# Interleaved gate and up weights, layer norms on one engine, and a later start of the PLE product in a 32-expert block

## The chip, the cores and the metric

The program runs on one core of one Trainium2 chip. Its time is the device time of one execution, in microseconds. The kernel before takes 2994.66 us, the median of three runs (2991.4 to 3000.03). The engines are named as in the profile: PE is TensorE, DVE is VectorE, ACT is ScalarE, POOL is GpSimd, SP is SyncE, which here only issues loads.

## The reference

Sequence length 256, width 2048, fp32. A first block (a mixer of an RWKV7 and an mLSTM branch, a mixture of experts, two layer norms) is followed by two further layers and a final norm. The change lies in the first block behind the mixer:

```
x = layer_norm(ALPHA * x + mix @ w_out, ln1_w, ln1_b)
moe = hier_moe(x, ...)          # 4 groups x 8 experts, top 1 group, top 2 experts
    # per expert: (silu(x_e @ w_gate) * (x_e @ w_up)) @ w_down, weighted, added back
ple = sigmoid(x @ w_pg) * (p @ w_ple)
x = layer_norm(ALPHA * x + moe + ple, ln2_w, ln2_b)
```

with `layer_norm(x) = (x - mean) * rsqrt(var + 1e-5) * w + b`. `w_gate` and `w_up` are 2048x512 for each of the 32 experts, `w_down` is 512x2048, `w_pg` 2048x2048, `w_ple` 256x2048. The weights of the experts alone are 403 million bytes.

## The kernel before, in words

Values that must keep fp32 accuracy outside the experts are split into a high and a low part (`split`, L316 the cast on ACT, L317 the difference on DVE or POOL), and a product is three matmuls (L220 to L222): high by high, low by high, high by low. A stream object (`st`) loads weight pieces of half a MB (`wraw`, L133), splits them (`whi`, `wlo`) and runs such products; `st.weave` mixes them with another generator's work.

The stages around the change: `out1` computes the output projection `mix @ w_out` from 32 loads (830 to 912 us), and adds x and the first statistics (L1082, L1083). `layer_norm` then works on two token tiles in four chunks of 512 columns: ACT scales and shifts (L1053), DVE multiplies by the weight (L1054), and POOL or DVE adds the bias (L1055). Each finished chunk is transposed (L1070), split (`xh`, `xl`), and multiplied by the router's weights (L1122 to L1124). `route` is a chain of small DVE operations; three small matmuls (L1201 to L1203) count the tokens of each expert, and a one-hot matrix (`oh`) follows.

`experts` works on four experts at a time: gather matmuls (L1327, `oh` by the rows' high part `zh` and low part `zl`) put up to 64 token rows of each expert in `xg`; then, per expert, gate and up (L1431), the activation, the down product (L1395) and the way back to the tokens (L1358, L1359). The weights come in blocks of 1 MB, twelve per expert (four gate, four up, four down), in the order that `expert_order` yields. A ring of eight buffers (`ew`) holds them, and two further blocks lie in `res`, free at that time. The ring's first eight blocks are issued from ACT's queue during `out1`; all others from SP's, each as soon as its buffer is free. A fp32 matmul of the program is recorded as two instructions. PLE (L220 to L222 on `xh`) is woven between the experts' steps, from the first expert on. At expert 24 stands a branch for tokens beyond the 64 rows (L1232), which is not taken. Behind the last expert come the second layer norm and the first norm of the next layer (L1684, `rdg`, a diagonal matrix of scales; L1691).

The order of the work within each engine is set when the program is built, by a scheduler that goes by buffers and the code's order; each queue then runs its list in order.

Of the kernel before, what the change touches and what calls it, by code (L numbers as in the profile page):

```python
# [9 lines left out]
F32 = mybir.dt.float32  # L10
F32R = mybir.dt.float32r
I32 = mybir.dt.int32
AF = mybir.ActivationFunctionType
# [252 lines left out]
class Ker:  # L266
# [767 lines left out]
    def ln_scale(self, pool, st, i, eps):  # L1034

        nc = self.nc
        mv = pool.tile([128, 2], F32, name="bmv")
        nc.vector.bn_aggr(mv, st[:, i])
        rs = pool.tile([128, 2], F32, name="brs")
        nc.vector.tensor_scalar_add(rs[:, 0:1], mv[:, 1:2], eps)  # L1040
        nc.gpsimd.tensor_tensor(rs[:, 0:1], rs[:, 0:1], self.mhalf, op=OP.pow)  # L1041
        nc.vector.scalar_tensor_tensor(rs[:, 1:2], mv[:, 0:1], -1.0, rs[:, 0:1], op0=OP.mult, op1=OP.mult)
        return rs[:, 0:1], rs[:, 1:2]

    def layer_norm(self, W2, z, st, w, b, eps, then):

        nc = self.nc
        scales = [self.ln_scale(W2, st, i, eps) for i in range(2)]
        for i, (rs, nm) in enumerate(scales):
            for c in range(4):  # L1050
                s = slice(512 * c, 512 * c + 512)
                v = z[:, i, s]
                nc.scalar.activation(v, v, AF.Identity, scale=rs, bias=nm)  # L1053
                nc.vector.tensor_mul(v, v, w[:, s])  # L1054
                (nc.vector if c % 2 else nc.gpsimd).tensor_add(v, v, b[:, s])  # L1055
                then(i, c)
# [153 lines left out]
    def overflow(self, EP, W2, acc, xh, xl, wt, pos, dram, hh, hl):  # L1210
# [21 lines left out]
        with tc.If(any_over > 0):  # L1232
            nc.sync.dma_start(dram.rearrange("e p a -> p a e"), wo)
            with tc.For_i(0, 32, 1) as e:
                gu = lambda n, c: lambda k0, kn: lambda raw: nc.sync.dma_start(
                    raw, A[n][bass.ds(e, 1), k0 // KCH, :, :, c:c + 256].rearrange("o p k n -> (o p) k n"))
                dn = lambda c, kp: lambda raw: nc.sync.dma_start(
# [4 lines left out]
                for c in range(0, 512, 256):  # L1242
                    h = EP.tile([128, 512], F32, name="plg0", bufs=1).rearrange("p (a s) -> p a s", a=2)

                    def ev_g(i, ps):
                        nc.scalar.activation(h[:, i], ps, AF.Silu)

                    def ev_u(i, ps):
                        nc.vector.tensor_mul(h[:, i], h[:, i], ps)
                        self.split(hh[:, i], hl[:, i], h[:, i])  # L1250

                    def ev_d(i, c, ps):
                        v = acc.t[:, i, 512 * c:512 * c + 512]
                        nc.vector.scalar_tensor_tensor(v, ps, wc[:, i:i + 1], v, op0=OP.mult, op1=OP.add)

                    st.cols_of(KT, 0, 256, xh, xl, ev_g, gu("w_gate", c))
                    st.cols_of(KT, 0, 256, xh, xl, ev_u, gu("w_up", c))
                    st.run()
                    st.rows(None, c // 256, 2, 0, D, hh, hl, ev_d, load=dn)
                    st.run()  # L1260

    def expert_order(self):
# [12 lines left out]
        for e in range(32):  # L1275
            for k in range(4):
                yield A["w_gate"][e, k]
                yield A["w_up"][e, k]
                if k == 1 and e:
                    yield from down(e - 1)  # L1280
# [12 lines left out]
    def load_expert(self, eng=None, t=None):  # L1293
        src = next(self.worder)
        t = self.wring.tile([128, 2048], F32, name="ew") if t is None else t
        v = t.rearrange("p (k n) -> p k n", n=src.shape[2])
        if src.shape[1] == 4:
            (eng or self.nc.sync).dma_start(t, src.rearrange("p k n -> p (k n)"))
        else:
            (eng or self.nc.sync).dma_start(v, src)  # L1300
        return v

    def experts(self, pool, W2, zp, x1, acc, wt, pos, bst):
# [6 lines left out]
        def load():  # L1310
            return self.wready.pop(0) if self.wready else self.load_expert()
# [98 lines left out]
        for e in range(32):  # L1410
            j = e % 4
            if j == 0:
                oh, xg, step = gather(e)
                step(0)
                if e == 0:
                    self.st.after = None
                sw = slot_weights(e, oh)
                yield
                if e == 24:
                    yield from self.start_overflow()  # L1420
# [4 lines left out]
            for k0 in range(0, KT, 4):  # L1425
                wg = load()
                wu = load()
                for w, ps in ((wg, acc_t[:, 0:256]), (wu, acc_t[:, 256:512])):
                    for k in range(4):
                        for g in range(2):  # L1430
                            nc.tensor.matmul(ps[64 * g:64 * g + 64], xg[:, k0 + k, j], w[:, k, 256 * g:256 * g + 256],  # L1431
                                             start=w is wg and k0 + k == 0, stop=k0 + k == KT - 1,
                                             tile_position=(0, 64 * g), skip_group_check=True)
                if j == 0 and k0 + 4 < KT:
# [608 lines left out]
def body(tc, A, out):  # L2043
# [13 lines left out]
    with ExitStack() as top:  # L2057
# [84 lines left out]
        with ExitStack() as pb:  # L2142
            psum(pb, 4)
            rp = pool(pb, "route")
            st.open(pool(pb, "ringB"), raw=2, split=2)
            xp = pool(pb, "xB")
            xh, xl = xp.tile([128, KT, S], F32R, name="xh"), xp.tile([128, KT, S], F32R, name="xl")
            ph, pl = xp.tile([128, 2, S], F32R, name="ph"), xp.tile([128, 2, S], F32R, name="pl")
            EP = pool(pb, "ex1")
            zh = xp.tile([128, 2, D], F32R, name="zh")  # L2150
            with ExitStack() as e:
# [14 lines left out]
                K.layer_norm(W2, z, bst, lw, lb, 1e-5, then)  # L2166
                st.after = [K.last_split]
                for c in range(4):
                    for i in range(2):
                        v = slice(512 * c, 512 * c + 512)  # L2170
                        nc.scalar.copy(zh[:, i, v], z[:, i, v])
                res = []
                st.weave(K.route(rp, R, lg, res))
                wt, pos = res
            K.ple(acc, EP, xh, xl, ph, pl)
            W2 = pool(pb, "ex2", bufs=2)
            zl = W2.tile([128, 2, D], F32R, name="zl", bufs=1)
            acc.x1 = zh, zl
            for c in range(4):
                for i in range(2):  # L2180
                    v = slice(512 * c, 512 * c + 512)
# [63 lines left out]
def prep(inp):  # L2245
# [41 lines left out]
    for n in ("w_out", "w_pg", "w_ple"):  # L2287
        a[n] = _by_rows(f(n)[0])
    for n in ("w_gate", "w_up"):
        a[n] = f(n)[0].reshape(32, 4, 4, 128, 512).transpose(0, 1, 3, 2, 4)  # L2290
    w = f("w_in_even_2")[0]
# [40 lines left out]
```

## Time and profile before

| | |
|---|---|
| median of three runs | 2994.66 us |
| profiled execution | 2988.51 us, its span 2986.6 us |
| PE busy | 2805.2 us (94%) |
| DVE, ACT, POOL busy | 55%, 38%, 17% |
| DMA over the span | 744.96 MB, 249 GB/s mean |
| DMA slices at 0.9 or more | from about 950 to 1970 us, the expert stage |

PE's busy time includes matmuls that are spread out by their operands, so the 94% is not an engine at its peak. The row of DMA slices shows the stage that the change is about: outside it, the DMA engines are busy for one to eight tenths, inside it for nine or more. In a row of windows the columns are the stretch, its length, the busy time of PE, PE's weight loads, DVE, ACT and POOL (with the number of instructions), PE's granted clock as a share of full speed, the share in which the 16 DMA engines were busy, and GB/s. In a row of the timeline they are the start, the time taken, the engine (SPq is SP's queue of loads), the line, the operation, what it writes and reads with shapes, how many follow each other, and in brackets the idle time before with the instruction or load that ended it.

### The profile page before, as it was taken

What the parts mean: (1) busy time and instruction counts of PE and PEld (TensorE: products, weight loads), DVE (VectorE), ACT (ScalarE), POOL (GpSimd) and SP (SyncE); (2) the same over time, 40 slices, a digit from 0 to 9 for tenths busy, and PEclk for the clock granted to TensorE, in tenths of its full rate; (3) what the DMA queues carried; (4) which work ended last, traced back from release to release, by engine and by line L of the source; (5) the groups of instructions that cost most, each with busy time, mean ns of one, the idle gap of its engine ahead of it and who ended that gap; (6) DMA issues with size and microseconds to landing.
All of it is one profiled execution on the core that took longest, in us unless ns stands there. A gap on an engine that the chain in (4) does not pass through costs nothing. (4 is left out here: it accounts for less than half of the span.)

```text
span 2986.6 us, 42995 instructions
## 1 busy us (share of the span) xinstructions
PE 2805.2 (94%) x16907; PEld 2068.6 (69%) x16907; DVE 1654.7 (55%) x2642; ACT 1138.7 (38%) x1959; POOL 516.2 (17%) x530
## 2 busy tenths in 40 slices
PE   8999899988998999999999899869889999999998
PEld 7877787876886555555555445447667787888887
DVE  7876865888666322222232222169999665555555
ACT  5443434555544212112112111044545554555454
POOL 4111102277103000000000000026675200000000
PEclk9999899999999999999999999989999999999999
DMA  6442142475684999999999999945555454555554
GB/s 195 135 132 71 53 147 96 163 254 198 225 310 175 404 415 398 419 417 386 419 419 413 418 396 419 419 186 185 165 168 166 170 202 157 186 180 188 181 180 166
DMA packets 170526, 744.96 MB, mean 249 GB/s; under 512 B 20544, under 2 KB 35408, under 8 KB 120784
## 3 DMA queue, kind: packets, MB, share of 16 engines
q1 hardware_dynamic: 162800, 719.09, 64.4%
q10 hardware_dynamic: 6624, 19.93, 1.8%
q0 software_dynamic: 896, 3.15, 0.4%
q8 instruction: 135, 2.21, 0.3%
q14 instruction: 71, 0.58, 0.1%
HBM read 727.40 MB, written 14.70 MB: 248 GB/s over the span
## 5 line engine op out<-in xcount | busy, mean ns | idle before, releaser
L155 PE MATMUL acc<-xx,whi 128*128 128x512 f32 (+2 forms) x2624 | 945.3, 403 | 16.9 <-ACT whi L316 11.3
L317 DVE TENSOR_TENSOR wlo<-wraw,whi 128x1024 fp32r<-128x1024 f32 x559 | 717.3, 1285 | 365.3 <-ACT whi L316 362.1
L159 PE MATMUL acc<-xx,wlo 128*128 128x256 f32 (+2 forms) x2624 | 729.3, 288 | 44.6 <-DVE wlo L317 44.5
L316 ACT CAST whi<-wraw 128x1024 fp32r<-128x1024 f32 x564 | 589.3, 1046 | 459.8 <-PE acc L222 224.2
L155 PEld LDWEIGHTS acc<-xx,whi 128*128 128x128 f32 (+2 forms) x2624 | 490.4, 190 | 123.8 <-ACT whi L316 11.8
L159 PEld LDWEIGHTS acc<-xx,wlo 128*128 128x128 f32 (+2 forms) x2624 | 499.5, 190 | 82.4 <-DVE wlo L317 62.2
L1431 PE MATMUL acc<-ew,xg 128*64 128x256 f32 x4064 | 482.2, 385 | 23.6 <-DMA ew<-in_w_gate 10.7
L1431 PEld LDWEIGHTS acc<-ew,xg 128*64 128x64 f32 x4064 | 282.1, 137 | 202.2 <-issue 34.8
L1369 DVE TENSOR_TENSOR z<-mx,z 64x512 fp32r<-64x512 f32 x128 | 86.7, 688 | 429.5 <-ACT z L1368 427.9
L1395 PE MATMUL mx<-ew,eht 128*64 128x512 f32 x992 | 228.6, 598 | 13.8 <-DMA ew<-in_w_down 13.8
L1368 ACT CAST z<-mx 64x512 fp32r<-64x512 f32 x128 | 74.1, 580 | 380.8 <-PE mx L1395 363.4
L1041 POOL TENSOR_TENSOR brs<-brs,mhalf 128x1 f32<-128x1 f32 x4 | 2.7, 671 | 1097.4 <-DVE brs L1040 1097.4
L1395 PEld LDWEIGHTS mx<-ew,eht 128*64 128x64 f32 x992 | 66.5, 136 | 142.9 <-issue 105.9
L166 ACT COPY halves<-acc 128x256 f32<-128x256 f32 x204 | 74.3, 366 | 215.2 <-PE acc L155 213.4
L221 PE MATMUL acc<-wlo,xx 128*128 128x512 f32 x256 | 102.1, 399 | 3.9 <-DVE wlo L317 3.9
L1376 DVE SCALAR_TENSOR_TENSOR eh<-eh,sw,acc 128x256 f32<-128x256 f32 x32 | 15.3, 480 | 159.7 <-ACT eh L1375 159.7
L222 PE MATMUL acc<-whi,xx 128*128 128x512 f32 x256 | 101.3, 396 | 0.0
L221 PE MATMUL acc<-wlo,oo 128*128 128x512 f32 x256 | 100.0, 391 | 0.0
L222 PE MATMUL acc<-whi,oo 128*128 128x512 f32 x256 | 99.5, 389 | 0.0
L220 PE MATMUL acc<-whi,xx 128*128 128x512 f32 x256 | 95.8, 397 | 0.0
L220 PE MATMUL acc<-whi,oo 128*128 128x512 f32 x256 | 93.1, 390 | 0.6 <-DVE res L1930 0.6
L168 DVE TENSOR_TENSOR halves<-halves,acc 128x256 f32<-128x256 f32 x148 | 61.1, 413 | 56.5 <-ACT halves L166 55.9
(614 smaller groups left out, 4056.1 us busy)
## 6 DMA issues: line engine op xcount, KB each, us to landing
ew<-in_w_down SPq DMA_DIRECT2D x128, 1024.0 KB, 14.3
ew<-in_w_gate SPq DMA_DIRECT2D x123, 1024.0 KB, 13.5
ew<-in_w_up SPq DMA_DIRECT2D x123, 1024.0 KB, 13.4
wraw<-in_wo_qkz SPq DMA_DIRECT2D x96, 512.0 KB, 3.3
wraw<-in_w_g SPq DMA_DIRECT2D x64, 512.0 KB, 3.3
wraw<-in_w_rkv SPq DMA_DIRECT2D x52, 512.0 KB, 3.6
wraw<-in_we_u SPq DMA_DIRECT2D x48, 512.0 KB, 3.5
wraw<-in_w_out SPq DMA_DIRECT2D x32, 512.0 KB, 5.2
```

Of the source, the lines that this page charges most:

```text
L155: nc.tensor.matmul(ps, p.hi[:, k], x.both(kk), start=kk == 0, stop=last, skip_group_check=True)
L159: nc.tensor.matmul(ps[:, 0:S], p.lo[:, k], x.h[:, kk], start=False, stop=False, skip_group_check=True)
L166: nc.scalar.copy(v, ps[:, S:])
L220: nc.tensor.matmul(acc[i], xh[:, kk, m], p.hi[:, k], start=kk == 0, stop=False)
L221: nc.tensor.matmul(acc[i], xh[:, kk, m], p.lo[:, k], start=False, stop=False)
L222: mm = nc.tensor.matmul(acc[i], xl[:, kk, m], p.hi[:, k], start=False, stop=last)
L316: self.last_split = self.nc.scalar.copy(hi, src).ins
L317: (eng or self.nc.vector).tensor_sub(lo, src, hi.bitcast(F32))
L1368: m = nc.scalar.copy(o[:, 0], v).ins
L1369: nc.vector.tensor_sub(o[:, 1], v, o[:, 0].bitcast(F32))
L1395: nc.tensor.matmul(py[b][64 * g:64 * g + 64, :], ht[:, k % 2, k // 2], wd[:, 0, c:c + 512], start=k == 0, stop=k == 3, tile_position=(0, 6 ...
L1431: nc.tensor.matmul(ps[64 * g:64 * g + 64], xg[:, k0 + k, j], w[:, k, 256 * g:256 * g + 256], start=w is wg and k0 + k == 0, stop=k0 + k == ...
```

## The change

The gate and up weights of an expert are stored as eight blocks of 1 MB, each with two slices of 128 rows and, for either half of the columns, 256 gate columns beside 256 up columns. A matmul covers 512 columns instead of 256, and there are half as many. The layer norm is two DVE operations for each chunk, `(x - mean) * w` and `(...) * rs + b`; the rows' low parts `zl` come from DVE too. PLE is started at the third expert, with its buffers opened there. Two more blocks are loaded ahead, into a pool `pre`. The branch stands at expert 28.

```diff
-        for i, (rs, nm) in enumerate(scales):
+        for i, (mean, rs) in enumerate(scales):
             for c in range(4):
...
-                nc.scalar.activation(v, v, AF.Identity, scale=rs, bias=nm)
-                nc.vector.tensor_mul(v, v, w[:, s])
-                (nc.vector if c % 2 else nc.gpsimd).tensor_add(v, v, b[:, s])
+                nc.vector.scalar_tensor_tensor(v, v, mean, w[:, s], op0=OP.subtract, op1=OP.mult)
+                nc.vector.scalar_tensor_tensor(v, v, rs, b[:, s], op0=OP.mult, op1=OP.add)
                 then(i, c)
...
         for e in range(32):
-            for k in range(4):
-                yield A["w_gate"][e, k]
-                yield A["w_up"][e, k]
-                if k == 1 and e:
+            for k in range(8):
+                yield A["w_gu"][e, k]
+                if k == 3 and e:
                     yield from down(e - 1)
...
         for e in range(32):
             j = e % 4
+            if e == 2:
+                self.start_ple()
             if j == 0:
                 oh, xg, step = gather(e)
                 step(0)
-                if e == 0:
-                    self.st.after = None
...
-                if e == 24:
+                if e == 28:
                     yield from self.start_overflow()
...
-                wg = load()
-                wu = load()
-                for w, ps in ((wg, acc_t[:, 0:256]), (wu, acc_t[:, 256:512])):
-                    for k in range(4):
-                        for g in range(2):
-                            nc.tensor.matmul(ps[64 * g:64 * g + 64], xg[:, k0 + k, j], w[:, k, 256 * g:256 * g + 256],
...
+                for k in range(k0, k0 + 4):
+                    w = load() if k % 2 == 0 else w
+                    for g in range(2):
+                        nc.tensor.matmul(acc_t[64 * g:64 * g + 64], xg[:, k, j], w[:, k % 2, 512 * g:512 * g + 512],
+                                         start=k == 0, stop=k == KT - 1, tile_position=(0, 64 * g))
...
-            st.open(pool(pb, "ringB"), raw=2, split=2)
+            px = ExitStack()
+            pre = pool(px, "pre", bufs=2, side="right")
+            K.wready += [K.load_expert(t=pre.tile([128, 2048], F32, name="pre")) for _ in range(2)]
...
-                st.after = [K.last_split]
                 for c in range(4):
                     for i in range(2):
                         v = slice(512 * c, 512 * c + 512)
-                        nc.scalar.copy(zh[:, i, v], z[:, i, v])
+                        K.split(zh[:, i, v], zl[:, i, v], z[:, i, v])
...
-            K.ple(acc, EP, xh, xl, ph, pl)
...
-                    nc.gpsimd.tensor_sub(zl[:, i, v], z[:, i, v], zh[:, i, v].bitcast(F32))
+            def start_ple():
+                px.close()
+                st.open(pool(pb, "ringB", side="right"), raw=2, split=2)
+                K.ple(acc, EP, xh, xl, ph, pl)
...
-            for _ in range(2):
-                with tc.issue_after(K.mark):
-                    st.step()
```

On SP's queue, from the loads of the output projection (`w_out`) to the first loads of the experts, the order before was:

```order
L133 DMA wraw<-in_w_out 128x1024 x27
L1298 DMA res<-in_w_gate 128x2048
L1298 DMA res<-in_w_up 128x2048
L133 DMA wraw<-in_w_pg 128x1024 x8
L1298 DMA ew<-in_w_gate 128x2048
L1298 DMA ew<-in_w_up 128x2048
L1300 DMA ew<-in_w_down 128x2048 x4
```

In the changed kernel it is:

```order
L133 DMA wraw<-in_w_out 128x1024
L1301 DMA pre<-in_w_gu 128x2048 x2
L133 DMA wraw<-in_w_out 128x1024 x26
L1301 DMA res<-in_w_gu 128x2048 x2
L1304 DMA ew<-in_w_down 128x2048 x4
L1301 DMA ew<-in_w_gu 128x2048 x4
L133 DMA wraw<-in_w_pg 128x1024 x2
```

The two new blocks stand ahead of 26 loads of `w_out`, and the eight first pieces of `w_pg`, which stood ahead of the ring's refill, stand behind eight blocks of it.

The same queue at the end of the experts, with the second norm's weights (`lnw`, `lnb`), before:

```order
L1298 DMA ew<-in_w_up 128x2048
L1300 DMA ew<-in_w_down 128x2x1024 x4
L1031 DMA lnw<-in_ln_w 128x2048
L1031 DMA lnb<-in_ln_b 128x2048
L133 DMA wraw<-in_we_u 128x1024
```

In the changed kernel, behind the branch (L1230):

```order
L1230 UNCONDITIONAL_BRANCH
L1031 DMA lnw<-in_ln_w 128x2048
L1031 DMA lnb<-in_ln_b 128x2048
L1301 DMA ew<-in_w_gu 128x2048 x5
L133 DMA wraw<-in_we_u 128x1024 x3
L1301 DMA ew<-in_w_gu 128x2048 x3
L1304 DMA ew<-in_w_down 128x2048 x4
```

The two loads moved from behind the last expert load to a place ahead of the last four experts' blocks.

On PE, from the last of the router's logits (`lt`) through the counts (`chosen`) to the first gathers (`oh`), the order before ends so:

```order
L220 MATMUL acc<-whi,xh 128x512 x2
L1327 MATMUL mx<-oh,zh 128x256 x2
L1340 MATMUL mx<-wt,oh 64x1 x2
L1327 MATMUL mx<-oh,zh 128x256
L1340 MATMUL mx<-wt,oh 64x1 x4
L1327 MATMUL mx<-oh,zl 128x256
```

In the changed kernel:

```order
L1126 MATMUL mx<-ident,lt 128x36
L1199 MATMUL mx<-chosen,low 128x32
L1200 MATMUL mx<-chosen,ones 128x32
L1201 MATMUL mx<-chosen,low 128x32
L1331 MATMUL mx<-oh,zh 128x256
L1331 MATMUL mx<-oh,zl 128x256
```

Of the PLE matmuls (L220 to L222), 50 stood between the logits and the first gathers; none does now, and the next instruction behind the logits is the first count.

## Rows read from the trace of the kernel before

**Rows 1.** Windows of the expert stage.

```profile
955.00:990.00 35.00, 35.00 (x293) 24.82 (x292) 5.78 (x8) 6.92 (x11) 5.97 (x4) 1.00 0.84 316
1105.00:1145.00 40.00, 39.50 (x247) 22.85 (x247) 11.23 (x14) 7.53 (x11) 0.00 (x0) 1.00 0.97 373
1145.00:1335.00 190.00, 183.37 (x1259) 106.78 (x1257) 49.08 (x76) 33.77 (x55) 0.00 (x0) 1.00 1.01 419
1335.00:1390.00 55.00, 55.00 (x337) 31.01 (x335) 14.99 (x20) 15.96 (x21) 0.00 (x0) 1.00 0.94 371
1390.00:1600.00 210.00, 203.92 (x1420) 118.57 (x1418) 54.31 (x84) 40.65 (x65) 0.00 (x0) 1.00 1.01 419
1711.00:1714.00 3.00, 2.66 (x10) 1.14 (x10) 0.00 (x0) 0.00 (x0) 0.00 (x0) 0.50 1.01 412
1720.00:1725.00 5.00, 5.00 (x42) 2.68 (x38) 0.00 (x0) 0.00 (x0) 0.00 (x0) 1.00 0.31 95
1725.00:1955.00 230.00, 206.27 (x1415) 107.44 (x1414) 49.94 (x82) 28.57 (x54) 0.00 (x0) 0.99 1.01 419
```

**Rows 2.** Timeline of PE at the end of the expert stage.

```profile
1949.43 1.95 PE L1431 MATMUL acc<-ew,xg 128*64 128x256 f32 x16 [0.55 <-DMA ew<-in_w_gate]
1951.94 1.95 PE L1431 MATMUL acc<-ew,xg 128*64 128x256 f32 x16 [0.56 <-DMA ew<-in_w_up]
...
1989.83 8.79 PE L1691 MATMUL mx<-rdg,res 128*128 128x128 f32 x64 [16.14 <-DVE rdg L1684]
```

**Rows 3.** Timeline of DVE in the routing ahead of the first gather.

```profile
938.55 2.31 DVE L1151 TENSOR_TENSOR rge<-lg,rgm 128x8 f32<-128x8 f32 x1
...
942.25 0.17 DVE L1151 TENSOR_TENSOR r1e<-ls,r1m 128x16 f32<-128x16 f32 x1
...
943.80 1.22 DVE L317 TENSOR_TENSOR wlo<-wraw,whi 128x1024 fp32r<-128x1024 f32 x1
```

**Rows 4.** Timeline of PE: first gathers, behind the branch, and a down product.

```profile
951.37 0.40 PE L1327 MATMUL mx<-oh,zh 128*128 128x256 f32 x2
...
957.22 1.08 PE L1431 MATMUL acc<-ew,xg 128*64 128x256 f32 x8
...
965.54 6.26 PE L1431 MATMUL acc<-ew,xg 128*64 128x256 f32 x56
...
1711.34 0.45 PE L1382 MATMUL mx<-ident,eh 128*128 128x128 f32 x1 [4.85 <-PEq L1232]
1711.72 1.98 PE L1431 MATMUL acc<-ew,xg 128*64 128x256 f32 x8
...
1935.87 5.52 PE L1395 MATMUL mx<-ew,eht 128*64 128x512 f32 x24
```

**Rows 5.** The output projection: its window, and ACT's waits from 826 to 912.

```profile
830.00:890.00 60.00, 60.00 (x267) 49.62 (x266) 32.38 (x32) 24.01 (x24) 0.00 (x0) 1.00 0.90 324
...
ACT whi L316 <- DMA wraw<-in_w_out: 30.6, 15, 4.3
```

**Rows 6.** Timeline of SP's queue: PLE pieces, behind the branch, the second norm.

```profile
914.81 45.39 SPq L133 DMA_DIRECT2D wraw<-in_w_pg  x8
...
1723.39 0.33 SPq L1298 DMA_DIRECT2D ew<-in_w_gate  x1
...
1973.77 0.34 SPq L1031 DMA_DIRECT2D lnb<-in_ln_b  x1
```

**Rows 7.** Timeline of DVE and POOL in the two layer norms.

```profile
911.25 0.69 DVE L1082 SCALAR_TENSOR_TENSOR z<-z,acc 128x512 f32<-128x512 f32 x1 [3.13 <-PE acc L222]
...
1974.93 0.27 DVE L1040 TENSOR_SCALAR brs<-bmv 128x1 f32<-128x1 f32 x2
...
1976.78 6.05 DVE L1054 TENSOR_TENSOR res<-res,lnw 128x512 f32<-128x512 f32 x6 [0.37 <-ACT res L1053]
...
1989.48 0.28 DVE L1684 TENSOR_SCALAR rdg<-ident,rrs 128x128 f32<-128x128 f32 x1 [0.72 <-POOL rrs L1063]
...
1978.33 3.34 POOL L1055 TENSOR_TENSOR res<-res,lnb 128x512 f32<-128x512 f32 x2 [2.11 <-DVE res L1054]
```

More of the change, by code (lines that the diff above doesn't have):

```diff
@@ L1038, in ln_scale @@
         nc.vector.bn_aggr(mv, st[:, i])
[L1039 to L1043, printed above, removed]
+        rs = pool.tile([128, 1], F32, name="brs")
+        nc.vector.tensor_scalar_add(rs, mv[:, 1:2], eps)
+        nc.gpsimd.tensor_tensor(rs, rs, self.mhalf, op=OP.pow)
+        return mv[:, 0:1], rs
     def layer_norm(self, W2, z, st, w, b, eps, then):
@@ L1234, in overflow, with gu, rows @@
             with tc.For_i(0, 32, 1) as e:
-                gu = lambda n, c: lambda k0, kn: lambda raw: nc.sync.dma_start(
-                    raw, A[n][bass.ds(e, 1), k0 // KCH, :, :, c:c + 256].rearrange("o p k n -> (o p) k n"))
+                def gu(n, c):
+                    def rows(raw, k):
+                        o = 2 * c + 256 * n
+                        v = A["w_gu"][bass.ds(e, 1), k // 2].rearrange("o p (k n) -> (o p) k n", k=2)
+                        nc.sync.dma_start(raw, v[:, :, o:o + 256])
+                    return lambda k0, kn: lambda raw: [rows(raw[:, k:k + 2], k0 + k) for k in range(0, kn, 2)]
                 dn = lambda c, kp: lambda raw: nc.sync.dma_start(
@@ L1254, in ev_d @@
                         nc.vector.scalar_tensor_tensor(v, ps, wc[:, i:i + 1], v, op0=OP.mult, op1=OP.add)
-                    st.cols_of(KT, 0, 256, xh, xl, ev_g, gu("w_gate", c))
-                    st.cols_of(KT, 0, 256, xh, xl, ev_u, gu("w_up", c))
+                    st.cols_of(KT, 0, 256, xh, xl, ev_g, gu(0, c))
+                    st.cols_of(KT, 0, 256, xh, xl, ev_u, gu(1, c))
                     st.run()
@@ L1295, in load_expert @@
         t = self.wring.tile([128, 2048], F32, name="ew") if t is None else t
+        if len(src.shape) == 2:
+            (eng or self.nc.sync).dma_start(t, src)
+            return t.rearrange("p (k n) -> p k n", k=2)
         v = t.rearrange("p (k n) -> p k n", n=src.shape[2])
[L1297 to L1300, printed above, removed]
+        (eng or self.nc.sync).dma_start(v, src)
         return v
@@ L1425, in experts @@
             for k0 in range(0, KT, 4):
-                wg = load()
-                wu = load()
-                for w, ps in ((wg, acc_t[:, 0:256]), (wu, acc_t[:, 256:512])):
-                    for k in range(4):
-                        for g in range(2):
-                            nc.tensor.matmul(ps[64 * g:64 * g + 64], xg[:, k0 + k, j], w[:, k, 256 * g:256 * g + 256],
-                                             start=w is wg and k0 + k == 0, stop=k0 + k == KT - 1,
-                                             tile_position=(0, 64 * g), skip_group_check=True)
+                for k in range(k0, k0 + 4):
[3 more added lines that the diff above has]
+                                         start=k == 0, stop=k == KT - 1, tile_position=(0, 64 * g))
                 if j == 0 and k0 + 4 < KT:
@@ L2149, in body @@
             EP = pool(pb, "ex1")
-            zh = xp.tile([128, 2, D], F32R, name="zh")
+            zh, zl = (xp.tile([128, 2, D], F32R, name=n) for n in ("zh", "zl"))
+            acc.x1 = zh, zl
             with ExitStack() as e:
@@ L2174, in body @@
                 wt, pos = res
-            K.ple(acc, EP, xh, xl, ph, pl)
             W2 = pool(pb, "ex2", bufs=2)
[L2177 to L2181, printed above, removed]
-                    nc.gpsimd.tensor_sub(zl[:, i, v], z[:, i, v], zh[:, i, v].bitcast(F32))
+            def start_ple():
+                px.close()
+                st.open(pool(pb, "ringB", side="right"), raw=2, split=2)
+                K.ple(acc, EP, xh, xl, ph, pl)
+            K.start_ple = start_ple
             K.start_overflow = lambda: K.overflow(EP, W2, acc, xh, xl, wt, pos, wov, ph, pl)
             bst = accp.tile([128, 2, 4, 6], F32, name="bst2")
-            for _ in range(2):
-                with tc.issue_after(K.mark):
-                    st.step()
             st.weave(K.experts(EP, W2, zp, (zh, zl), acc, wt, pos, bst), per=0.7)
@@ L2288, in prep @@
         a[n] = _by_rows(f(n)[0])
-    for n in ("w_gate", "w_up"):
-        a[n] = f(n)[0].reshape(32, 4, 4, 128, 512).transpose(0, 1, 3, 2, 4)
+    w = np.stack([f(n)[0].reshape(32, 8, 2, 128, 2, 256) for n in ("w_gate", "w_up")], 5)
+    a["w_gu"] = np.ascontiguousarray(w.transpose(0, 1, 3, 2, 4, 5, 6)).reshape(32, 8, 128, 2048)
     w = f("w_in_even_2")[0]
```

## The prediction

> **What bounds the kernel now.** I read the windows by stage first, since a busy share over the whole span mixes stages with different limits. The change touches three: the output projection (830 to 912 us), the 32 experts (951 to 1973), and the second layer norm behind them. In the expert stage the DMA engines are full: share 1.01 and 419 GB/s in the long stretches, while TensorE is busy for 89.7% of 1725 to 1955 [rows 1]. TensorE's timeline at the stage's end shows it block by block: sixteen matmuls take 1.95 us, then the engine waits 0.55 us for the next block, and blocks start 2.51 us apart [rows 2]. That is the time of 1 MB (1.0486 million bytes) at 419 GB/s, 2.50 us. So the end of this stage is fixed by bytes, by how many blocks were ahead when the loads became continuous, and by the dips in which the loads stopped. There are three dips that matter: 1105 to 1145, 1335 to 1390 and 1720 to 1725 [rows 1]. In the first two TensorE is busy for 39.50 of 40 and all of 55 us; there it held the buffers, and the loads waited for it. The third is the branch. In the output projection TensorE is busy for 60.00 of 60 us [rows 5]; behind the experts it stands idle for 16.14 us for the norm [rows 2].
>
> **A, the start of the experts.** Before, the first gather matmul starts at 951.37 [rows 4]. Three things ahead of it go. A DVE operation of the routing beside GpSimd's weight split takes 2.31 us, where the same line alone takes 0.17: 2.1 us. Two DVE weight splits (one is shown, 1.22 us, with a short overlap at its end) stand between routing operations: 2.3 us [rows 3]. And TensorE had PLE matmuls in its queue ahead of the routing's count matmuls and of the gathers; for the waits behind them, on DVE and on TensorE, I estimate 2.5 us, some eleven such matmuls at 60.00 / 267 = 0.225 us [rows 5]. The norm itself I put at no gain: DVE now does all of it. That gives a first gather at about 944.5. From there to the first expert matmul it was 5.85 us, with some thirty gathers and three PLE matmuls in between; now eighteen gathers stand there, and I estimate 3.4 us: 947.9 instead of 957.22 [rows 4].
>
> What is that worth? Not 9 us, since the loads and not TensorE set the end. By blocks: before, ten were loaded ahead, an estimated three blocks' worth of PLE pieces (six of the eight half blocks that SP issues from 914.81 on [rows 6]) had followed by 955, and 955 to 990 moved 35 us x 316 GB/s = 11.06 MB, 10.5 blocks [rows 1]: 23.5 at 990. After, twelve are ahead. A block frees its buffer when its matmuls are done: 16 recorded instructions of 256 columns before, at 6.26 / 56 = 0.11 us, so 1.8 us [rows 4]. But four of the first twelve blocks are not in the ring and free nothing, so only six more loads can land by about 969, and the loads are continuous from about 973, when 18 blocks are in. At 990 that makes 18 + 17 / 2.50 = 24.8. The lead is 1.3 blocks, 3.2 us.
>
> Two costs stand against it. TensorE no longer has PLE matmuls while it waits for the routing. After 4.85 us of idle time at the branch its granted clock was 0.50, the 1.2 GHz level, from 1711 to 1714 [rows 1], and the next two batches of eight matmuls took 1.98 us each, where such a batch takes 1.08 otherwise [rows 4]: 1.8 us. The idle stretch will be about 7 us here, so I take that. The Trainium skill ("TensorE: Matmul & The Clock Gate", Part 1, "What's actually happening") says the same of an engine that was idle; the rows at the branch agree, and the sum holds no more than they show.
>
> The other is the two blocks loaded on SP's queue ahead of 26 of the output projection's 32 loads. TensorE is never idle there, but ScalarE waits 30.6 us in 15 waits for those loads, and the window's DMA share is 0.90 [rows 5]. Two blocks are 5.0 us of DMA time; with no slack they delay the projection by all of it, with enough by nothing. TensorE's 60.00 of 60 is the nearer row: I take 1. So A = -3.2 + 1.8 + 1 = **-0.4 us**, between -3.2 (no cold start, no delay) and +6.8 (no lead, both costs at 1.8 and 5).
>
> **B, the second norm's weights.** The two loads stood behind the last expert load, the second at 1973.77 [rows 6]. Now they come right behind the branch, ahead of the blocks of the last four experts, in a stretch at 419 GB/s. Two blocks at 2.50 us: **+5.0 us** on the last expert load. What hid them before was idle DMA.
>
> **C, the branch.** Before, SP issued nothing until 1723.39 [rows 6], and 1720 to 1725 moved 95 GB/s instead of 419: 5 x 324 / 419 = 3.9 us lost [rows 1]. Now the first load behind the branch waits until everything before it has landed, so the queue runs empty once for certain. One load alone went from 1973.77 to the first GpSimd addition that uses it at 1978.33 [rows 6, 7]: 4.6 us at most, of which 2.5 are its bytes. So 2.1 lost instead of 3.9: **-1.8 us** (bounds -3.9 and 0).
>
> **D, the PLE dips.** Before, 53 of the 432 PLE matmuls run ahead of the experts, in time in which TensorE had nothing else. Now all 432 lie between the third expert and about the twenty-second: 53 x 0.225 = 11.9 us more for TensorE, at the projection's pace [rows 5]. In 1145 to 1335 and 1390 to 1600 it has 6.6 + 6.1 = 12.7 us without work [rows 1], which would just hold them. If none fits: +11.9. If the dips vanish instead: 40 x 46 / 419 + 55 x 48 / 419 = 4.4 + 6.3, that is -10.7. The long stretches with room are the nearer rows; I let the dips recur and a sixth of the new work not fit: **+2 us**.
>
> Does the wide matmul give room? A recorded 256-column instruction takes about 0.11 us in a stream and a 512-column one 0.23 (5.52 us for 24) [rows 4]: twice the columns, twice the time. So no.
>
> **E, the second norm.** From 1974.93 to the scale matrix at 1989.48 it took 14.55 us, with DVE at 1.0 us a multiplication beside GpSimd's additions [rows 7]. Now 16 scalar-tensor-tensor operations follow on DVE. Such a one over 128x512 took 0.69 [rows 7]: from 1975.2 to 1986.2, and 0.8 for the last sum and power: 1987.0, **-2.5 us**. At 1.0 us each it would be +2.5; at a start-to-start of 0.6 it would be -3.9. GpSimd has no large operation left there, so 0.69.
>
> **Sum.** -0.4 + 5.0 - 1.8 + 2 - 2.5 = +2.3 us. The profiled execution took 2988.51 us, span 2986.6: 2990.8 in its frame. It lies 6.2 us under the median of the three runs, 2994.66, to which the forecast refers: **2997.0 us**. What a measurement of this kernel can tell from no change is 0.3%, 9 us.
>
> **Rivals.**
> R1, faster: TensorE gets room and the dips go. The Trainium skill ("TensorEngine Tiling (Array Packing)", "Instruction Overhead") gives each matmul about 60 cycles on top of its columns; by that, the 2048 recorded gate and up instructions that go would give TensorE an estimated 51 us (25 ns each at 2.4 GHz) over the stage. The rows on either width speak against it (0.11 and 0.23). But dips can also go because twelve blocks ahead and PLE two experts later give a better phase, with the routing's wait shorter. For it: the long stretches have the room. Against it: 100% busy in one dip, and 11.9 us more work. D is then -10.7 instead of +2, and the lead keeps its 3.2 without the 2.8 of A's two costs: 2997.0 - 12.7 - 2.8 = 2981.5.
> R2, slower: TensorE becomes the bound from expert 3 to 22. For it: 96.5% and 97.1% busy in the two long stretches, 100% in one dip [rows 1]. Against it: the ring evens out some microseconds. It decides as soon as the 11.9 us find no room; D is +11.9 instead of +2: 3006.9.
> R3, the start does not do what it says: DVE alone does 16 norm operations and 16 splits, the logits come later by what the routing gains, the lead of 3.2 is lost, and the two early blocks cost 5 instead of 1: 2997.0 + 7.2 = 3004.2.
>
> **Chances.** Forecast 0.42 (its own range 2989 to 3003), R1 0.30, R2 0.20, R3 0.08. Faster by over 0.3% (under 2985.7): R1 and a little of the forecast's tail, 0.31. Slower by over 0.3% (over 3003.6): R2 and half of R3, 0.24. The rest is 0.45. The range takes in R1 and R2, with some microseconds beside R1: 2978 to 3008.
>
> **What would show it.** The first gather at 944 to 945 with the clock at half for about 3 us (A); the norm's weights issued right behind the branch, and the last gate and up block later by B, C and D less A's lead (before: 1951.94) (B, C); windows of the PLE stretch with shares under 1.0 at a TensorE near 100% (D; all at 1.01: R1; a stretch of hundreds of us under 1.0: R2); 12 us from the last statistics to the first matmul of the even layer (E). TensorE idle between 830 and 912 shows the early blocks' price. I would be wrong most of all if the wide matmuls ran faster per column than the narrow ones.

## The result, and the profile after

The changed kernel takes 3011.17 us (median of four runs, 3008.77 to 3016.12) against 2994.98 us before: the ratio is 1.0056, 95% interval 1.0044 to 1.0067. It is slower, and outside the range of the prediction. The profiled execution has a span of 3008.3 us, against 2986.6. These spans differ by 21.7 us and the medians by 16.2, because the profiled execution of the kernel before lies 6.5 us under the median of its runs and that of the changed kernel 1.2 under.

Three marks divide the loss: the first aggregated statistics of the first layer norm (L1038 on DVE), which end the output projection; the last gate and up block; and the first matmul behind the second norm.

| mark | before | after | difference |
|---|---|---|---|
| first statistics | 912.70 | 925.14 | 12.4 |
| last gate and up block | 1951.94 | 1977.79 | 25.9 |
| first matmul behind the second norm | 1989.83 | 2012.59 | 22.8 |
| span | 2986.6 | 3008.3 | 21.7 |

Of the 21.7 us, 12.4 have arisen before the first expert, 13.5 more come within the experts, and some 4 are won back behind them. Of the 12.4, some 4.7 are not the change's: in the eleven kernels below whose projection is as before, the first statistics came at 914.8 to 921.3 in their profiles, 917.4 in the mean, and before's 912.70 is the earliest of all. In the table of the experiments, times are counted from that mark. Its rows, before and after:

```profile
912.70 0.27 DVE L1038 BATCH_NORM_AGGREGATE bmv<-bst 128x2 f32<-128x24 f32 x1
```

```profile
925.14 0.26 DVE L1038 BATCH_NORM_AGGREGATE bmv<-bst 128x2 f32<-128x24 f32 x1
```

The output projection first. These are two windows of the changed kernel, and ScalarE's waits for loads from 826 to 925 (the columns of a wait are the total, the count and the longest); both answer to [rows 5]:

```profile
830.00:890.00 60.00, 54.92 (x230) 44.40 (x229) 32.05 (x36) 21.84 (x24) 1.65 (x3) 0.94 0.82 301
...
853.00:856.00 3.00, 2.96 (x7) 2.15 (x7) 2.74 (x3) 1.30 (x2) 0.00 (x0) 0.50 0.89 309
```

```profile
ACT whi L316 <- DMA wraw<-in_w_out: 35.9, 14, 9.3
```

SP's queue, ScalarE and TensorE at that place, from their timelines:

```profile
835.59 0.85 SPq L1301 DMA_DIRECT2D pre<-in_w_gu  x2
836.74 76.60 SPq L133 DMA_DIRECT2D wraw<-in_w_out  x26
...
850.99 1.04 ACT L316 CAST whi<-wraw 128x1024 fp32r<-128x1024 f32 x1 [9.30 <-DMA wraw<-in_w_out]
...
852.08 1.22 PE L220 MATMUL acc<-whi,mh 128*128 128x512 f32 x2 [5.04 <-ACT whi L316]
...
853.93 0.63 PE L222 MATMUL acc<-whi,ml 128*128 128x512 f32 x1
854.36 0.63 PE L220 MATMUL acc<-whi,mh 128*128 128x512 f32 x1
```

The two early blocks are issued at 835.59. ScalarE waits 9.30 us for the next piece of the projection's weights, where its longest such wait before was 4.3 [rows 5]; TensorE stands idle for 5.04 us, and then its matmuls follow each other at 0.43 us instead of 0.225 until 858.63, at a granted clock of 0.50, the 1.2 GHz level (853 to 856). So the idle stretch is paid for once more in part, by slow matmuls behind it.

Then the start of the experts, the stage's end and the second norm (TensorE, SP and VectorE), answering to [rows 2, 4, 6, 7]:

```profile
956.73 0.55 PE L1331 MATMUL mx<-oh,zh 128*128 128x256 f32 x1 [0.87 <-DVE oh L1321]
...
962.14 1.92 PE L1433 MATMUL acc<-ew,xg 128*64 128x512 f32 x8
...
1956.32 5.37 PE L1433 MATMUL acc<-ew,xg 128*64 128x512 f32 x24
...
1977.79 1.94 PE L1433 MATMUL acc<-ew,xg 128*64 128x512 f32 x8 [0.57 <-DMA ew<-in_w_gu]
...
2012.59 7.59 PE L1692 MATMUL mx<-rdg,res 128*128 128x128 f32 x52 [13.40 <-DVE rrs L1060]
```

```profile
926.40 0.80 SPq L1301 DMA_DIRECT2D res<-in_w_gu  x2
964.10 11.19 SPq L1304 DMA_DIRECT2D ew<-in_w_down  x4
...
1865.43 0.34 SPq L1031 DMA_DIRECT2D lnw<-in_ln_w  x1
1865.82 0.42 SPq L1031 DMA_DIRECT2D lnb<-in_ln_b  x1
```

```profile
950.20 0.17 DVE L1149 TENSOR_TENSOR rge<-lg,rgm 128x8 f32<-128x8 f32 x1
...
2000.47 0.15 DVE L1040 TENSOR_SCALAR brs<-bmv 128x1 f32<-128x1 f32 x1
...
2005.89 5.38 DVE L1053 SCALAR_TENSOR_TENSOR res<-res,brs,lnb 128x512 f32<-128x512 f32 x8
...
2012.24 0.29 DVE L1685 TENSOR_SCALAR rdg<-ident,rrs 128x128 f32<-128x128 f32 x1
```

From the first statistics to the first gather it is 31.6 us instead of 38.7, as predicted. But nothing is loaded between the blocks in `res` and 964.10, when the first expert frees a buffer. The last fence has the routing's operation that took 2.31 us [rows 3] and now takes 0.17, and the end of the second norm.

The loads then stop once more. SP's queue again (rows from 977 to 980 and from 985 to 989), TensorE, and the window:

```profile
977.26 2.04 SPq L1301 DMA_DIRECT2D ew<-in_w_gu  x2
987.81 0.33 SPq L1301 DMA_DIRECT2D ew<-in_w_gu  x1
```

```profile
980.70 3.22 PE L1433 MATMUL acc<-res,xg 128*64 128x512 f32 x13
```

```profile
985.00:990.00 5.00, 5.00 (x26) 1.73 (x24) 0.05 (x1) 0.38 (x1) 0.00 (x0) 1.00 0.23 59
```

The second of the two loads at 977.26 is issued at 978.97, and none follows for 8.8 us: from 980.70 TensorE works on blocks in `res` and `pre`, which free no buffer of the ring. From 985 to 990 only 59 GB/s are moved, 5 x 360 / 419 = 4.3 us lost.

In the expert stage itself the loads lose more in dips than before. Windows of the changed kernel, which answer to [rows 1], and in the second fence the same stretches with TensorE's time for one of PLE's three lines alone (L221; the other two are as many), which shows where PLE's matmuls lie:

```profile
1000.00:1055.00 55.00, 55.00 (x223) 23.89 (x221) 22.65 (x33) 9.56 (x15) 0.00 (x0) 1.00 1.01 418
1055.00:1100.00 45.00, 44.04 (x241) 21.30 (x238) 9.38 (x14) 13.46 (x20) 0.00 (x0) 1.00 0.96 366
1100.00:1155.00 55.00, 52.20 (x236) 18.15 (x234) 12.29 (x20) 6.95 (x13) 0.00 (x0) 1.00 1.01 420
...
1245.00:1270.00 25.00, 25.00 (x101) 11.09 (x102) 5.83 (x8) 4.14 (x5) 0.00 (x0) 1.00 0.86 322
...
1640.00:1675.00 35.00, 35.00 (x149) 14.17 (x149) 7.26 (x10) 9.88 (x13) 0.00 (x0) 1.00 0.88 335
1860.00:1870.00 10.00, 10.00 (x54) 4.45 (x52) 0.00 (x0) 1.17 (x2) 0.00 (x0) 1.00 0.47 194
```

```profile
1000.00:1055.00 55.00, 9.41 (x23) 4.33 (x23) 1.00 1.01 418
1055.00:1100.00 45.00, 3.55 (x9) 1.69 (x9) 1.00 0.96 366
1100.00:1155.00 55.00, 0.00 (x0) 0.00 (x0) 1.00 1.01 420
1155.00:1245.00 90.00, 8.29 (x21) 3.95 (x21) 1.00 1.01 418
1245.00:1270.00 25.00, 4.45 (x11) 2.07 (x11) 1.00 0.86 322
```

PLE does not lie evenly between the experts. It comes in four bursts of about 100 matmuls, with stretches between them in which there is next to none, and towards the end of a burst the loads fall off. The last row of the first fence is the branch.

In the kernel before, too, TensorE's idle time lay where PLE did not. Two windows of it, and the same two for L221 alone:

```profile
1180.00:1290.00 110.00, 104.55 (x760) 58.07 (x758) 26.11 (x43) 18.08 (x32) 0.00 (x0) 1.00 1.01 419
1290.00:1335.00 45.00, 45.00 (x299) 29.11 (x297) 11.40 (x16) 8.26 (x12) 0.00 (x0) 1.00 1.01 418
```

```profile
1180.00:1290.00 110.00, 0.00 (x0) 0.00 (x0) 1.00 1.01 419
1290.00:1335.00 45.00, 8.87 (x22) 4.14 (x22) 1.00 1.01 418
```

Of the 6.6 us of idle time between 1145 and 1335 [rows 1], 5.45 lie in the first of these, between two bursts, and none in the second, where the third burst begins.

### The profile page after: what moved, and what is told of

It is laid out like the page before. It is cut to its first block, busy times and chain, and to the rows that moved or that the text cites. A ratio compares the mean times of both kernels' runs of the same rounds, so it can differ in the third digit from the quotient of the medians.

```text
span 3008.3 us, 38879 instructions
## 1 busy us (share of the span) xinstructions
PE 2812.9 (94%) x14859; PEld 1923.0 (64%) x14859; DVE 1649.5 (55%) x2656; ACT 1124.9 (37%) x1941; POOL 488.2 (16%) x512
## 5 line engine op out<-in xcount | busy, mean ns | idle before, releaser
L1433 PE MATMUL acc<-ew,xg 128*64 128x512 f32 x2016 | 479.1, 604 | 26.4 <-DMA ew<-in_w_gu 20.4
L1433 PEld LDWEIGHTS acc<-ew,xg 128*64 128x64 f32 x2016 | 133.4, 137 | 293.6 <-issue 222.7
L221 PE MATMUL acc<-wlo,xx 128*128 128x512 f32 x256 | 102.9, 402 | 4.3 <-DVE wlo L317 4.3
L222 PE MATMUL acc<-whi,xx 128*128 128x512 f32 x256 | 101.9, 398 | 0.0
L221 PE MATMUL acc<-wlo,oo 128*128 128x512 f32 x256 | 100.0, 391 | 0.0
L222 PE MATMUL acc<-whi,oo 128*128 128x512 f32 x256 | 99.5, 389 | 0.0
L220 PE MATMUL acc<-whi,xx 128*128 128x512 f32 x256 | 96.1, 398 | 0.0
L220 PE MATMUL acc<-whi,oo 128*128 128x512 f32 x256 | 93.1, 390 | 0.5 <-DVE res L1931 0.5
```

Source lines behind the costliest of these rows:

```text
L220: nc.tensor.matmul(acc[i], xh[:, kk, m], p.hi[:, k], start=kk == 0, stop=False)
L221: nc.tensor.matmul(acc[i], xh[:, kk, m], p.lo[:, k], start=False, stop=False)
L222: mm = nc.tensor.matmul(acc[i], xl[:, kk, m], p.hi[:, k], start=False, stop=last)
L1433: nc.tensor.matmul(acc_t[64 * g:64 * g + 64], xg[:, k, j], w[:, k % 2, 512 * g:512 * g + 512], start=k == 0, stop=k == KT - 1, tile_positi ...
```

## The experiments

Each ran in five rounds beside the kernel before (2994 to 2996 us in the three sets). The two columns of lost time are worked out from windows of 5 us, as (419 - GB/s) / 419 x 5, summed over the stretches with a clear dip; the times in the last two columns count from the first statistics; blocks are the MB moved in the first 100 us behind that mark, divided by 1.0486. A kernel has one profiled execution, and the median is of other executions too.

| kernel | median, ratio (interval) | blocks at +100 | lost in PLE's stretch | lost at the branch | last gate and up block | first matmul behind the norm |
|---|---|---|---|---|---|---|
| before | 2994.98 | 24.7 | 10.5 | 3.9 | 1039.2 | 1077.1 |
| changed | 3011.17, 1.0056 (1.0044, 1.0067) | 22.2, and 2 earlier | 18.8 | 5.4 | 1052.7 | 1087.4 |
| e1 | 3005.97, 1.0039 (1.0027, 1.0051) | 24.0 | 19.2 | 5.1 | 1052.4 | 1087.2 |
| e2 | 3000.95, 1.0019 (1.0010, 1.0029) | 24.0 | 18.6 | 5.1 | 1052.8 | 1087.9 |
| e3 | 2991.06, 0.9990 (0.9981, 0.9999) | 24.8 | 11.1 | 4.6 | 1037.3 | 1075.3 |
| e4 | 2987.14, 0.9975 (0.9964, 0.9986) | 25.8 | 11.7 | 4.6 | 1037.9 | 1073.2 |
| e5 | 2986.18, 0.9972 (0.9963, 0.9982) | 25.7 | 11.2 | 4.3 | 1034.7 | 1070.0 |
| e6 | 2997.38, 1.0011 (1.0002, 1.0020) | 24.8 | 16.2 | 4.3 | 1045.6 | 1083.6 |
| e7 | 3000.00, 1.0022 (1.0010, 1.0034) | 24.1 | 18.9 | 4.6 | 1046.9 | 1082.1 |
| e9 | 2984.97, 0.9967 (0.9956, 0.9978) | 24.2 | none | 6.9 | 1034.9 | 1070.2 |
| e10 | 2980.16, 0.9947 (0.9935, 0.9960) | 23.6 | none | 6.1 | 1029.9 | 1064.8 |
| e11 | 2985.09, 0.9967 (0.9955, 0.9980) | 24.3 | none | 6.5 | 1029.1 | 1064.2 |
| e12 | 2992.56, 0.9991 (0.9981, 1.0000) | 22.1, and 2 earlier | none | 6.3 | 1035.3 | 1070.1 |
| e13 | 2992.03, 0.9991 (0.9982, 1.0000) | 21.8 | none | 6.1 | 1037.4 | 1075.4 |

**e1, the two early blocks behind the projection.**

```diff
-            K.wready += [K.load_expert(t=pre.tile([128, 2048], F32, name="pre")) for _ in range(2)]
+            pret = [pre.tile([128, 2048], F32, name="pre") for _ in range(2)]
...
                     lw, lb = (K.bcast_row(L, A["ln1_" + n], "ln" + n, nc.scalar) for n in "wb")
+                    K.wready += [K.load_expert(nc.scalar, t) for t in pret]
```

> The changed kernel, but the two extra blocks (pre) are issued from ScalarE's queue behind the norm's weights, so behind every load of the output projection, instead of ahead of 26 of them on SP's queue. Theory T1 (the two early blocks stall the projection: in the trace TensorE lost 5.0 us there, then ran at the low clock, and the first norm began 8.6 us later than the offset before that explains): TensorE is busy 60 of 60 us from 830 to 890 again, everything behind moves 8.6 us forward, 3011 - 8.6 = about 3003 us, ratio 1.0027. Rival T1b (the expert stage's end is set by bytes and dips in which loads stop, so an earlier start is given back there): 3011 us, ratio 1.0056. Rival T1c (late, the two blocks compete with the norm's weights and delay the norm): 3006 us or more.

Its window shows that the stall is gone (ScalarE's longest wait for a load is 5.0 us):

```profile
830.00:890.00 60.00, 59.24 (x259) 47.96 (x258) 34.22 (x36) 24.34 (x25) 0.99 (x2) 1.00 0.86 309
```

The first statistics come 9.0 us earlier in the profile than in the changed kernel, and from there on the two are equal. The medians differ by 5.2 us. T1 holds; T1b does not, since no part of the start was given back in the stage; and the first gather comes 31.6 us behind the statistics as in the changed kernel, so the norm is not delayed (T1c). The profiled execution of e1 is the fastest of its six, so the size is open between 5 and 9.

**e2, no early blocks at all** (the line of `pre` and its pool left out).

> The changed kernel without the two extra blocks and their pool: ten blocks are ahead. PLE's buffers then have free room, and its first four pieces of half a MB are loaded behind the blocks in res, in the time in which the ring waits for the first expert. T1: the stall of 8.6 us goes, the two blocks (5.0 us) must be loaded in the full stage, but the four pieces (also 5.0 us) come out of it: about 3003 us, ratio 1.0027. Rival T1b (the start is given back in the stage): 3011 us. Rival T1d (the two blocks themselves are worth their 5 us and the pieces are not, since PLE starts two experts later anyway): 3008 us.

10 us less than the changed kernel. Behind the first statistics its trace runs as e1's does: the two blocks and the four PLE pieces are worth the same there, as T1 said. The median is 5 us under e1's, which the traces do not show (its profiled execution, at 3008.11 us, is the slowest of its twelve, e1's the fastest of its six), and the intervals of the two ratios overlap.

**e3, interleaved weights alone**, the diff's parts on `w_gu`, `load_expert` and the gate and up matmuls.

> The kernel before with the gate and up weights interleaved and 512-column matmuls, and nothing else. Theory T2 (twice the columns take twice the time, bytes are the same): 2995 us, ratio 1.000 within 0.0015. Rival T2b (TensorE gains room and the dips of the loads in the PLE stretch go): about 2984 us, ratio 0.9964. Rival T2c (a matmul of 512 columns holds up others, or the block of both gate and up frees its buffer later, and dips grow): 3002 us or more, ratio 1.0025.

3.4 us faster, barely clear of nothing. The dips are as before (11.1 us lost, 10.5 before), and TensorE's busy time over the whole span falls by 4.5 us, from 2805.2 to 2800.7: the wide matmul gives it next to no room.

**e4, both norms on VectorE alone**, the diff's `ln_scale` and `layer_norm`.

> The kernel before with both layer norms as two VectorE operations for each chunk, and nothing else (low parts on GpSimd, PLE from the first expert, narrow matmuls). Theory T3 (the second norm gains 2.8 us as in the changed kernel's trace, the first ends at the same time): 2995 - 2.8 = 2992 us, ratio 0.9991. Rival T3b (the first norm on VectorE alone delays the routing): 2997 us or more, ratio over 1.0005.

7.3 us faster (4.2 to 10.8 by the interval), more than either theory. Its trace shows 3.9 us from the first statistics to the first matmul behind the second norm. The second norm accounts for 2.6 of them (35.3 instead of 37.9 from the last block to the first matmul behind it). The first norm gives a lead: the first gather comes 35.6 us behind the first statistics instead of 38.7, and 1.1 blocks more are in at +100, 2.8 us, of which the larger dips take 1.9 back. In the changed kernel VectorE computes the rows' low parts there too, and the logits are ready after 24.6 us as against 25.4 before.

**e5, e3 and e4 together.**

> The kernel before with two parts of the change together: interleaved gate and up weights with 512-column matmuls, and both norms on VectorE. PLE starts with the first expert, low parts of the rows on GpSimd, no extra blocks ahead. Theory T4 (the loss of the changed kernel comes from the late start of PLE, from the place of the second norm's weights and from the early blocks, and these two parts are gains that add up): 0.999 x 0.9975 = 0.9965, about 2984 us. Rival T4b (the two parts gain on the same wait): 2987 us, ratio 0.9975. Rival T4c (together with the wide matmuls the loss shows up): 2994 us or more.

8.6 us faster, between T4 and T4b. So these parts of the change are gains together, and what follows has to explain some 25 us of loss.

**e6, PLE from the third expert alone** (with the branch at expert 28, and the places of the first pieces and of the norm's weights pinned).

```diff
+            if e == 2:
+                self.start_ple()
...
-                if e == 24:
+                if e == 28:
...
+            def start_ple():
+                st.after = None
+                st.open(pool(pb, "ringB"), raw=2, split=2)
+                K.ple(acc, EP, xh, xl, ph, pl)
```

> The kernel before with PLE started at the third expert and the branch at expert 28, and nothing else: its first four pieces are loaded behind the blocks in res, the second norm's weights behind the last expert block as before. Theory T4 (the 53 PLE matmuls that ran ahead of the experts make the first burst of PLE as heavy as the others, and dips in which loads stop grow by about 8 us; the start loses what PLE's pieces filled): about 2994 + 12 = 3006 us, ratio 1.004. Rival T4d (the late start costs only what the dips show): 3002 us, ratio 1.0027. Rival T4e (neutral; the loss needs the wide matmuls or the low parts on VectorE): 2995 us.

2.6 us slower, between T4d and T4e. The trace shows the mechanism, lost time 16.2 instead of 10.5, with the stage 6.4 us longer; the time shows less than that.

**e7, the second norm's weights behind the last block again**, on top of e1.

```diff
-                lw, lb = K.bcast_row(L, A["ln2_w"], "lnw"), K.bcast_row(L, A["ln2_b"], "lnb")
+                with tc.issue_after(K.last_load):
+                    lw, lb = K.bcast_row(L, A["ln2_w"], "lnw"), K.bcast_row(L, A["ln2_b"], "lnb")
```

> The changed kernel with the extra blocks behind the projection (as in e1), and with the second norm's two weight loads behind the last expert block again. Theory (two blocks of 2.50 us in a full stage cost 5.0 us): 5 us less than e1, 3001 us, ratio 1.0022. Rival (the loads are then late for the norm, which waits for them): 3006 us, ratio 1.0039, with VectorE waiting for a load behind the statistics.

6.0 us less than e1 between the medians, though the intervals of the two ratios overlap, and 5.5 us in the stage's end in the trace; the norm doesn't wait for them. By the trace the price of two blocks is 5 us, as predicted.

**e9, PLE spread**, on top of e1: each PLE step is queued on TensorE behind the gate and up matmuls that come before it in the code.

```diff
             while due >= 1:
-                self.step()
+                with ExitStack() as es:
+                    if self.pace:
+                        es.enter_context(self.K.tc.issue_after(self.pace))
+                    self.step()
                 due -= 1
...
+                self.st.pace = mm.ins if e < 27 else None
```

> The changed kernel with the extra blocks behind the projection (as in e1), and with every PLE step queued on TensorE behind the gate and up matmuls that the program puts ahead of it: 6 to 12 PLE matmuls in each half expert from the third to the 27th, instead of four bursts of about 25 in each half expert with pauses between. The work is the same. Theory T5 (the loads stop because a burst asks for more TensorE time than a block's 2.50 us; 1.8 us of gate, up or down and up to 0.9 of PLE, with the gathers on top): spread out it fits, the dips of 19 us in e1 (5.8, 5.0, 1.7 and 6.7) go for the most part, 3006 - 15 = 2991 us, ratio 0.999; shares of 1.01 throughout. Rival T5b (TensorE has too much work over the whole stretch): the loads lose the same 19 us, spread out, 3006 us. Rival T5c (the forced order adds waits for PLE's split weights): 3010 us or more.

21 us less than e1, more than forecast; in the traces the last gate and up block comes 17.5 us earlier behind the first statistics. Its window from 990 to 1820, and two of the stretches in which the changed kernel had dips:

```profile
1055.00:1100.00 45.00, 45.00 (x210) 19.97 (x209) 11.98 (x18) 9.74 (x17) 0.00 (x0) 1.00 1.01 419
1245.00:1270.00 25.00, 22.43 (x96) 7.63 (x94) 3.44 (x6) 3.20 (x6) 0.00 (x0) 1.00 1.01 419
...
990.00:1820.00 830.00, 813.39 (x3879) 343.19 (x3875) 226.14 (x347) 154.65 (x248) 0.00 (x0) 1.00 1.01 419
```

In the changed kernel the same window has 409 GB/s, and so it has in e1:

```profile
990.00:1820.00 830.00, 801.97 (x3776) 339.39 (x3774) 224.74 (x342) 152.34 (x243) 0.00 (x0) 1.00 1.00 409
```

10 / 419 x 830 = 19.8 us. The same work in another order takes TensorE 98.0% of the stretch and lets the loads run through: T5 holds, T5b doesn't.

**e10, e5 with PLE spread.**

> e5 (the kernel before with interleaved weights and both norms on VectorE, PLE from the first expert) with PLE's matmuls queued behind the gate and up matmuls that the program puts ahead of them, as in e9: 6 to 12 in each half expert up to the 24th. Theory T5 (bursts of PLE make the dips): the dips of e5 (3.8, 6.6 and 0.8 us) go, 2986 - 11 = 2975 us, ratio 0.9935. Rival T5d (41 of the 53 matmuls that ran ahead of the experts now lie inside, 9 us, and fill TensorE): 2984 us, ratio 0.9965.

The fastest of all, 15.8 us under the kernel before. It lies between T5 and T5d: the dips go, but two blocks fewer than in e5 are in at +100. One of them is missing at +45 already (4.8 instead of 5.8), where fewer of PLE's pieces have been loaded ahead of the first expert; and from 990 to 995 the loads fall to 259 GB/s.

**e11, e9 with the norm's weights last.**

> e9 with the second norm's two loads behind the last expert block, as in e7. Theory (5.0 us of bytes in a full stage, whatever the dips): 2985 - 5 = 2980 us, ratio 0.995. Rival (without the dips the stage has slack elsewhere): 2985 us, ratio 0.9967.

The stage ends 5.8 us earlier in the trace, while the medians of e11 and e9 are equal. The intervals are 12 parts in 10,000 to either side, 4 us; that the 5 us are saved here too isn't shown by time. The layers behind the norm, which no run changes, took 998.2 us in e11's trace and 995.3 in e9's.

**e12, the changed kernel with PLE spread.**

> The changed kernel with PLE spread as in e9 and nothing else: the two extra blocks again ahead of 26 loads of the projection. Theory T1 (the early blocks stall the projection; e1 measured 5 us, its trace showed 9): 2985 + 5 to 9 = 2990 to 2994 us, ratio 0.9984 to 0.9997. Rival (the stall is given back in the stage once the dips are gone): 2985 us.

7.6 us over e9. With e1 that makes 5 to 8 us for the early blocks, and the rival falls (the two intervals do not meet). In the profile the first statistics come at 925.79, as late as in the changed kernel.

**e13, the kernel before with PLE spread.**

> The kernel before with PLE spread as in e9 and nothing else. Theory T5: the dips of before (3.9, 6.0 and 0.6 us) go, 2995 - 10 = 2985 us, ratio 0.9967. Rival T5d (fewer PLE matmuls run ahead of the experts, so the gain is given back): 2993 to 2996 us, ratio 0.9995 to 1.0003.

3.9 us faster between the medians, with an interval that reaches 1.0000, so barely told from nothing. In the trace both theories are half right: the dips are gone, and 2.9 blocks at 2.50 us, 7.2 us, are missing at +100.

## Why the prediction was wrong, step by step

The bound was read rightly: the stage ends when its bytes are in, and what counts are blocks ahead, added bytes and dips. The steps, with what the runs showed:

- **D, the dips: the step that failed most.** I took the 12.7 us of idle time in the two long stretches as room for the 11.9 us of added PLE matmuls, and +2. Lost time in PLE's stretch went from 10.5 to 18.8, so +8.3, seven tenths of the added 11.9 where I had let a sixth not fit. The idle time was real, but it lay between the bursts (5.45 of the first stretch's 6.6 us), and the work came inside them. Before, the second and the third of four bursts held a large dip, and the first, half of which ran ahead of the experts, none. Now the first, the second and the fourth end in one. e9 shows it from the other side. R2 had the place right and the reason wrong: TensorE was not short of time over the stretch, but for 50 us at a time.
- **A, the early blocks: mis-sized, and its bound was wrong.** I took 1 us, and 5 at most, the two blocks' bytes. It cost 5 to 8 us of time (e1, e12), and 7.8 in the trace (925.14 against the mean of 917.4). The wait itself kept to the bound, 5.04 us; what went beyond it in the trace is the slow clock behind: fourteen matmuls took 6.55 us that take 3.2 otherwise, together 8.4. I had priced that for the experts' start and not for the projection. The row that I went by, TensorE's 60.00 of 60 us, does not speak for slack: an engine that is busy throughout is the bound, and what it is made to wait is lost.
- **A, the lead: wrong.** I forecast 1.3 blocks more at the start of the saturated stretch. Counted at 100 us behind the first statistics it is 24.2 with the two early ones, against 24.7: half a block less, 1.2 us instead of -3.2. The first gather came when forecast (31.6 us behind the first statistics, forecast 944.5 - 912.7 = 31.8), and at +60 some 18 blocks were in, as forecast (10 loaded ahead and 8.1 behind the mark). The step that failed is that the loads would be continuous from there (973, +60): from +60 to +65, which is 985 to 990, only 0.3 blocks came, where 2.0 fit. I had counted the four blocks in `res` and `pre`, which free nothing, when I counted what can land, and not when TensorE would work on them. In the six traces with `pre`, 0.3 to 0.6 blocks came in that stretch, in the eight without it 1.1 to 2.0; e1 and e2, which differ in `pre`, stand at 9.8 and 9.1 blocks at +60 and both at 11.9 at +70. The cold clock at the gathers came as forecast: they follow each other at 0.21 us instead of 0.12 until 960.9, at a granted clock of 0.50 (957 to 960).
- **B, +5.0: right by the traces.** They show 5.5 (e7) and 5.8 (e11); in time e7 has 6.0 and e11 nothing, where the interval of each median is some 4 us to either side.
- **C, -1.8: wrong in sign, small.** The bubble lost 5.4 instead of 3.9. The queue ran empty as forecast, but for longer than the single load's latency that I had taken for it.
- **E, -2.5: right.** From the statistics' end to the first scale matrix it is 2012.24 - 2000.47 = 11.8 us instead of 14.55, -2.8. The eight last operations took 5.38, 0.67 each, against the 0.69 that I took.
- **The wide matmul: right for TensorE.** 24 recorded instructions of 512 columns in 5.37 us are 0.224 each, twice 0.112. The rule of about 60 cycles for each matmul ("TensorEngine Tiling (Array Packing)", "Instruction Overhead", in the Trainium skill) would have freed an estimated 51 us. In e3 TensorE's busy time fell by 4.5 us and the dips are as before, so this stream doesn't show it.

Behind the first statistics these parts add up to 1.2 + 8.3 + 5.0 + 1.5 - 2.8 = 13.2 us, where the two traces differ by 10.3 at the first matmul behind the norm. Counted by bytes the account closes. From +100 to the last gate and up block 386.7 MB are moved before and 388.9 after, 5.2 us more at 419 GB/s; what the stage takes beyond its bytes at that rate is 16.3 us before and 24.5 after, 8.2 more for all dips and the branch together; and from that block to the first matmul behind the norm it is 34.8 us instead of 37.9, -3.1. That makes 10.3. So D and C are 8.2 together rather than 9.8: the table leaves out small dips, of which the kernel before has more. The span's 21.7 are 4.7 ahead of all that the change touches, 7.8 for the early blocks, these 10.3, and -1.1 in the layers behind.

One thing stays open. e6 says that the late start of PLE alone costs 2.6 us, while e7 lies 13.8 over e5. In the traces e7 starts with 1.6 blocks fewer at +100 (4.0 us) and loses 7.7 us more in dips, which makes 11.7 of the 12.1 between their marks. The dry stretch from +60 to +65 is a part of the poorer start (0.6 blocks in e7, 1.4 in e5, 1.8 in e6); the rest was not tried.

## What to carry to other kernels

Idle time of an engine counts as room only where the added work will lie: look at how the filler work is spread over the stretch, not at the sum of its idle time. Where a stage is bound by transfers, order the filler evenly before thinking about how much of it there is; here the order alone was worth 21 us, more than the whole change cost. A transfer put ahead of others in a queue can cost more than its bytes, where the engine behind it stands still long enough to lose its clock (here 8.4 us in the trace for 5.0 us of bytes). And blocks loaded ahead into buffers outside the ring give a lead that can be lost again when their turn comes, since no buffer of the ring is freed then.

## What was not expected of the hardware

One idle stretch of 5.04 us cost TensorE another 3.4 us in slow matmuls: fourteen of them took 6.55 us, 852.08 to 858.63, instead of 3.2. TensorE at 98.0% busy for 830 us (e9) held no load up, while at 96.6% in bursts (the changed kernel) it did.
